# Hybrid decoder layer on one core: bank turn of the query projections, two scalars in the probability scaling, deferred last step of the output projection

## Chip, cores and metric

One core of one Trainium2 chip runs the whole program. The metric is the device time of one execution in microseconds (us), the median of several runs.

## What is computed

One decoder layer over 512 tokens of width 1024: a gated linear recurrence and a sparse attention in parallel, merged by two sigmoid gates, an output projection, an expert layer (16 experts of 16384 for each of 8 heads and token) and a gated embedding. The part that matters here, cut from the reference:

```
z_q, z_kv, z_ng, z_m = parts of rmsnorm(x) @ w_in
p_s = masked_softmax(q_rot @ k_s);  p_w = masked_softmax(q_rot @ k_w)
o_b = g0 * (p_c @ v_c) + g1 * (p_s @ v_s) + g2 * (p_w @ v_w)      # g = sigmoid(z_ng)
g_m = sigmoid(z_m).reshape(B, S, 2, D)
merged = g_m[:, :, 0] * y_a + g_m[:, :, 1] * (o_b @ w_b)
h = x + merged @ w_out
```

## The kernel before

Every float32 product is taken as three products of parts (hi x hi, hi x lo, lo x hi; `mm3`, lines 131 to 134). A part hi is a cast on ScalarE (line 126), a part lo a subtraction on VectorE or, for most weights, on GpSimd (line 129, both in `split`). Weights come in pieces of 512 KB through a ring of three raw buffers whose loads SyncE issues in a fixed order; a load waits until both readers of its buffer are done.

The order of the work is written out by hand, engine by engine, in the order of the Python code. Around the change it is this.

**Queries.** `gemm` projects eight pieces of queries. Each takes a PSUM bank from `bank`, whose tag goes round `"aaax"`: three banks under tag a, one (bank 3) under tag x. `ev_q` copies the piece on ScalarE and starts its rotation on VectorE (`rope`, lines 633 to 636, which read the bank); the scores against the compressed keys follow one piece later (line 658). During the pieces the first attention block takes two banks a for its scores.

**Merge gates.** `m_gemm` computes sixteen pieces of z_m as filler. It takes banks f and x in turn, eight steps of three matmuls to a piece. Its first twelve steps stand right behind the queries; the rest is spread between the steps of attention.

**Attention.** Sixteen blocks (128 tokens times two heads). For block n `att_a` makes scores, their maximum (line 754 or 751) and exponentials with sums (line 758); `att_a2` (lines 767 to 770) multiplies both branches of the probabilities P of one head by gate / sum. `att_b` of the block before, running at the same time, transposes its own P on TensorE (line 812), splits them into th and tl, and multiplies them with the values into bank o. Its last act is the split of o into ohi and olo (in the trace qhi and qlo, whose place they take). Head 0 of block n is scaled within `att_b(n - 1)`, head 1 behind it.

**Merge and output projection.** `gemm` with w_b gives eight pieces; `ev_yb` (lines 866, 867 and a split) makes mhi and mlo of each. Then w_out follows in four column groups q (lines 890 to 931): for each of four token tiles i, 16 matmuls with the hi weights over k = 0 to 7 (lines 914, 915), then for each i eight with the lo weights (line 898) and the addition to hres (line 900). Step k needs piece k of mhi and mlo. The weights of group q + 1 are cast behind tile 0.

```
def bank(name, tag="ax"):
    if tag == "ax":
        tag = "aaax"[turn[0] % 4]
        turn[0] += 1
    return ps.tile([128, 512], F32, name=name, tag=tag, bufs=NBK[tag])
```

Of the kernel before, what the change touches and what calls it, by code (L numbers as in the profile page):

```python
# [17 lines left out]
OP = mybir.AluOpType  # L18
# [5 lines left out]
NT = S // 128  # L24
KD = D // 128
# [69 lines left out]
def tile_hybrid(ctx, tc, a, out, dbg=None):  # L95
    nc = tc.nc
    V, A, T, G, SP = nc.vector, nc.scalar, nc.tensor, nc.gpsimd, nc.sync
# [15 lines left out]
    turn = [0]  # L113
# [7 lines left out]
    def f(ap):  # L121
        return ap.bitcast(F32)
# [21 lines left out]
    p1cm, p = enter(tc.tile_pool(name="p1", bufs=2, side="right"))  # L144
# [24 lines left out]
    ring = Ring(wp, nc, plan, 3)  # L169
# [367 lines left out]
    def pair_split(n, which, j, tiles):  # L537
        r = ring.get(n).rearrange("p (k c) -> p k c", k=KD)
        c = slice(j * 128, (j + 1) * 128)
        split(tiles[0][:, :, c], tiles[1][:, :, c], r, lo_eng[0])  # L540

    def pair(n):
        return [wp.tile([128, KD, 256], F32R, name="w8" + n + x, tag="w8") for x in "hl"]
# [32 lines left out]
    for br, n in enumerate(("vs", "vw")):  # L576
        hl = hls[br]
# [33 lines left out]
    gate = at.tile([128, NT, 24], F32, name="gate")  # L611
# [60 lines left out]
    def cmp_softmax_a(i, h0=0, h1=NH):  # L672
        s, m = pc[:, i, h0:h1], pm[:, 0, i, h0:h1]
        V.tensor_reduce(m, s, axis=AX.X, op=OP.max)
        V.tensor_tensor(s, s, m[:, :, None].to_broadcast([128, h1 - h0, NB]), op=OP.subtract)
        A.activation(s, s, AF.Exp, scale=SCALE)

    def cmp_softmax_b(i, h0=0, h1=NH):
        s, z, r = pc[:, i, h0:h1], pm[:, 1, i, h0:h1], pm[:, 2, i, h0:h1]
        V.tensor_reduce(z, s, axis=AX.X, op=OP.add)  # L680
        V.reciprocal(r, z)
        V.tensor_tensor(r, r, gate[:, i].rearrange("p (h b) -> p h b", b=3)[:, h0:h1, 0], op=OP.mult)
        if i == 0:
            V.tensor_scalar(r, r, cst[:, C_RM:C_RM + 1], None, op0=OP.mult)
        V.tensor_tensor(s, s, r[:, :, None].to_broadcast([128, h1 - h0, NB]), op=OP.mult)
# [76 lines left out]
    def att_a2(n, h):  # L762
        i, hp = blocks[n]
        W = (i + 1) * 128
        hh = hp * 2 + h
        P, st = Pt[n, h], stt.pop((n, h))
        V.reciprocal(st[:, 3], st[:, 2])
        V.tensor_tensor(st[:, 3], st[:, 3], gate[:, i, 3 * hh + 1:3 * hh + 3], op=OP.mult)
        for br in range(2):
            V.tensor_scalar(P[:, br, :W], P[:, br, :W], st[:, 3, br:br + 1], None, op0=OP.mult)  # L770

    def att_b(n, acts, more=None):
        i, hp = blocks[n]
        g = hp // 2
        oo = bank("o", "o")
        tiles = [(br, j) for br in range(2) for j in range(i + 1)]
        steps = [None] + [tiles[k:k + 2] for k in range(0, len(tiles), 2)]
        slots = [len(steps) + 2]
        half = slots[0] - max(1, int(slots[0] * PART))
        pend = []  # L780

        def gap():
            left = slots[0] - half
            if more and left == 0:
                acts.extend(more())
            for _ in range(-(-len(acts) // (left if left > 0 else slots[0]))):
                acts.pop(0)()
            slots[0] -= 1
            fill(1)

        def pv(k, last):
            js, th, tl = k
            if js is None:
                mm3(oo[:, :256], vchi[:NB, g], vclo[:NB, g], th[:NB, 0], tl[:NB, 0], True, last)
                return
            for m, (br, j) in enumerate(js):
                c = slice(g * 128, (g + 1) * 128)
                mm3(oo[:, :256], vhi[:, j, br, c], vlo[:, j, br, c], th[:, m], tl[:, m], False,
                    last and m == len(js) - 1)

        for js in steps:
            o = bank("pT", "t").rearrange("p (j x) -> p j x", j=2)
            th = p.tile([128, 2, 256], F32R, name="th", tag="th", bufs=3)
            tl = p.tile([128, 2, 256], F32R, name="tl", tag="tl", bufs=3)
            if js is None:
                for h in range(2):
                    T.transpose(o[:NB, 0, h * 128:(h + 1) * 128], pc[:, i, hp * 2 + h], ident)
                split(th[:NB, 0], tl[:NB, 0], o[:NB, 0])
            else:
                for m, (br, j) in enumerate(js):  # L810
                    for h in range(2):
                        T.transpose(o[:, m, h * 128:(h + 1) * 128], Pt[n, h][:, br, j * 128:(j + 1) * 128], ident)
                split(th[:, :len(js)], tl[:, :len(js)], o[:, :len(js)])
            gap()
            if len(pend) == 2:
                pv(pend.pop(0), False)
            pend.append((js, th, tl))
        while pend:
            gap()
            k = pend.pop(0)  # L820
            pv(k, not pend)
        oc = slice(hp * 2, hp * 2 + 2), slice(i * 128, (i + 1) * 128)
        split(ohi[:, oc[0], oc[1]], olo[:, oc[0], oc[1]], oo[:, :256].rearrange("p (h t) -> p h t", h=2))

# [7 lines left out]
        att_a2(0, 1)  # L832

    side += [lambda: None] * 3 + [att_0, lambda: cmp_softmax_a(0, 0, 4), lambda: cmp_softmax_b(0, 0, 4), att_02]
    gemm([("q", i, nhi, nlo, ev_q) for i in range(8)], nxt=[("m1", 0), ("m1", 1)])
    for _ in range(FILL0):
        next(fillg)
# [3 lines left out]
    for n in range(1, len(blocks) + 1):  # L841
        acts = []
        if n < len(blocks):
            acts = list(att_a(n, 0)) + [lambda: att_a2(n, 0)]
        cur[0] = blocks[n - 1][0]
        att_b(n - 1, acts, (lambda: att_a(n, 1)) if n < len(blocks) else None)
        if n < len(blocks):
            att_a2(n, 1)
            if n == 1:
                cmp_softmax_a(0, 4, 8)  # L850
                cmp_softmax_b(0, 4, 8)
            i, hp = blocks[n]
            if i + 1 < NT and hp in (2, 3):
                (cmp_softmax_a if hp == 2 else cmp_softmax_b)(i + 1)
# [15 lines left out]
    jobs = [("w_b", i, ohi, olo, ev_yb) for i in range(8)]  # L870
    gemm(jobs[:7], nxt=[("w_b", 7)])
    hl = pair("wo")
    for j in range(2):
        pair_split("w_out", None, j, hl)
    gemm(jobs[7:])

    p3cm, p = enter(tc.tile_pool(name="p3", bufs=2, side="left"))
    hres = at.tile([128, NT, D], F32, name="hres", tag="gm")
# [12 lines left out]
    for q in range(4):  # L891
        os = [bank("wo") for _ in range(NT)]
        nhl = None

        def wo_lo(i):
            ts = slice(i * 128, (i + 1) * 128)
            for k in range(KD):
                T.matmul(os[i][:, :256], mhi[:, k, ts], hl[1][:, k], start=False, stop=k == KD - 1)
            hv = hres[:, i, q * 256:(q + 1) * 256]
            V.scalar_tensor_tensor(hv, os[i][:, :256], 0.5, hv, op0=OP.mult, op1=OP.add)  # L900
            if q == 3:
                rms_stat(hres[:, i], i, x2s[:, i])
                rms_fin(i, i + 1)
                if i >= 1:
                    rms_apply(x2s[:, i - 1], hres[:, i - 1], i - 1, gB)
                if i >= 2:
                    to_T(x2s[:, i - 2], x2hi, x2lo, i - 2)

        if q < 3:
            nhl = pair("wo")  # L910
        for i in range(NT):
            ts = slice(i * 128, (i + 1) * 128)
            for k in range(KD):
                T.matmul(os[i][:, :256], mhi[:, k, ts], hl[0][:, k], start=k == 0, stop=False)
                T.matmul(os[i][:, :256], mlo[:, k, ts], hl[0][:, k], start=False, stop=False)
            if q == 3:
                wo_lo(i)
            if nhl and i == 0:
                for j in range(2):
                    r = ring.get("w_out", 2).rearrange("p (k c) -> p k c", k=KD)  # L920
                    A.copy(nhl[0][:, :, j * 128:(j + 1) * 128], r)
                    nhl.append(r)
        for i in range(NT):
            if q < 3:
                wo_lo(i)
            if nhl and i == 0:
                for j in range(2):
                    c = slice(j * 128, (j + 1) * 128)
                    G.tensor_tensor(nhl[1][:, :, c], nhl[2 + j], f(nhl[0][:, :, c]), op=OP.subtract)
        if q == 0:  # L930
            split(phl[:, 0], phl[:, 1], pw[:, 0].rearrange("p (k t) -> p k t", k=2), G, V)
        elif q < 3:
            split(wphl[:, 0, q - 1], wphl[:, 1, q - 1], pw[:, q], G, V)
        if q == 2:
            hi_eng[0] = V
            look([("wq", 0)])
        hl = nhl
# [654 lines left out]
```

## Time and profile before

| what | value |
|---|---|
| median of 3 runs | 1894.97 us (1893.92 to 1895.76) |
| the profiled execution's own time | 1896.81 us |
| its span in the trace | 1895.0 us |
| busy: TensorE, VectorE, ScalarE, GpSimd | 96%, 74%, 44%, 34% |
| queries / attention / w_b / w_out, about | 280 to 330 / 330 to 530 / 530 to 574 / 574 to 625 us |
| expert layer and end, about | 625 to 1895 us |

The chain that ended last runs over TensorE for 73% of the span. TensorE's queue is in order, so a matmul that waits holds all behind it. In the rows, PE is TensorE, PEld its weight load, DVE VectorE, ACT ScalarE, POOL GpSimd. A time in square brackets at the end of a row is how long the engine stood idle before it, and whose end it waited for.

### The profile page before, as it was taken

The page shows a single profiled execution, that of the slowest core. Times are in us where ns is not written, and L with a number is a line of the kernel's source. Part 1 is how long each engine was busy: PE and PEld are TensorE (multiplying, and loading weights), DVE is VectorE, ACT ScalarE, POOL GpSimd, SP SyncE. Part 2 cuts the span into 40 slices and gives each one's busy share as a digit, 9 for nine tenths or more (in the row PEclk, how much of TensorE's full clock was granted, in tenths as well). Part 3 has the DMA queues.
Part 4 walks back from the last instruction along what each step waited for, and adds up shares of the span by engine and source line. Part 5 has one row for each costly group of instructions (what it writes and reads, how often), then busy time and mean ns, then how long its engine had stood idle before and what let it go on. Part 6 is the DMA issues. An engine that isn't in the chain of part 4 may idle for free.

```text
span 1895.0 us, 26509 instructions
## 1 busy us (share of the span) xinstructions
PE 1819.3 (96%) x9817; PEld 1594.3 (84%) x9817; DVE 1401.5 (74%) x2658; ACT 840.3 (44%) x1274; POOL 648.8 (34%) x419
## 2 busy tenths in 40 slices
PE   7998999999999989999999999999999999999997
PEld 6777888777789879899999888888888899999986
DVE  6867607565633378999999967888888788888864
ACT  4464333344522434574674763333333333333443
POOL 3311454322135325335335321222222255556400
PEclk9999999899999999999999999999999999999999
DMA  4353232211015426697787998999999899999941
GB/s 171 105 183 97 89 101 67 67 56 45 23 67 178 190 87 202 233 365 257 275 331 258 335 357 298 355 358 352 347 355 353 304 338 324 348 337 350 363 178 45
DMA packets 179810, 433.29 MB, mean 229 GB/s; under 512 B 14560, under 2 KB 88032, under 8 KB 179680
## 3 DMA queue, kind: packets, MB, share of 16 engines
q1 hardware_dynamic: 119664, 241.96, 36.8%
q0 software_dynamic: 40288, 145.77, 21.5%
q10 hardware_dynamic: 19728, 43.86, 6.1%
q8 instruction: 77, 1.26, 0.3%
q14 instruction: 53, 0.43, 0.1%
HBM read 382.25 MB, written 49.28 MB: 228 GB/s over the span
## 4 chain that ended last, share of the span: by engine, by line
PE 73%; DVE 16%; ACT 4%; issue 4%; DMA 3%; POOL 0%; SPq 0%; DVEq 0%; ACTq 0%; POOLq 0%
PE va L132 9%; PE va L134 9%; PE va L133 9%; PE xu L134 7%; PE xu L132 7%; PE xu L133 7%; DVE ul L1087 2%; DVE oh L1259 2%; DVE gr L1288 1%; PE G L1236 1%; PE z_m L132 1%; PE z_m L133 1%; PE z_m L134 1%; DVE acc L1294 1%; PE sc L996 1%
## 5 line engine op out<-in xcount | busy, mean ns | idle before, releaser
L132 PE MATMUL xu<-x2hi,uh 128*128 128x384 f32 x1008 | 345.2, 342 | 4.7 <-ACT ac L1097 4.7
L134 PE MATMUL xu<-x2hi,ul 128*128 128x384 f32 x1008 | 340.6, 338 | 5.8 <-DVE ul L1087 5.8
L133 PE MATMUL xu<-x2lo,uh 128*128 128x384 f32 x1008 | 339.9, 337 | 0.0
L132 PE MATMUL va<-v,A 128*128 128x512 f32 x768 | 299.0, 389 | 1.5 <-ACT A L126 1.5
L134 PE MATMUL va<-v,A 128*128 128x512 f32 x768 | 298.8, 389 | 0.0
L133 PE MATMUL va<-v,A 128*128 128x512 f32 x768 | 298.8, 389 | 0.0
L1273 POOL DMA_INDIRECT gr<-in_peer_u,eidx x128 | 170.7, 1333 | 327.8 <-DVE gr L1288 250.5
L1273 POOL DMA_INDIRECT gr<-in_peer_v,eidx x128 | 187.8, 1467 | 267.5 <-DVE acc L1294 210.2
L126 ACT CAST v<-vring 128x1024 fp32r<-128x1024 f32 x128 | 134.7, 1052 | 262.7 <-issue 144.2
L129 DVE TENSOR_TENSOR v<-vring,v 128x1024 fp32r<-128x1024 f32 x128 | 156.5, 1223 | 67.8 <-ACT v L126 67.2
L132 PEld LDWEIGHTS xu<-x2hi,uh 128*128 128x128 f32 x1008 | 191.4, 190 | 7.0 <-ACT ac L1097 5.3
L134 PEld LDWEIGHTS xu<-x2hi,ul 128*128 128x128 f32 x1008 | 191.1, 190 | 6.8 <-DVE ul L1087 6.8
L133 PEld LDWEIGHTS xu<-x2lo,uh 128*128 128x128 f32 x1008 | 191.4, 190 | 1.6
L134 PEld LDWEIGHTS va<-v,A 128*128 128x128 f32 x768 | 144.1, 188 | 30.4 <-DVE A L129 0.3
L132 PEld LDWEIGHTS va<-v,A 128*128 128x128 f32 x768 | 144.1, 188 | 29.9 <-ACT A L126 1.8
L133 PEld LDWEIGHTS va<-v,A 128*128 128x128 f32 x768 | 144.1, 188 | 28.3
L1294 DVE SCALAR_TENSOR_TENSOR acc<-gr,dots,acc 128x1024 f32<-128x1024 f32 x128 | 164.0, 1281 | 2.2 <-DMA gr<-in_peer_v,eidx 0.7
L1288 DVE SCALAR_TENSOR_TENSOR gr<-gr,x2g 128x1024 f32<-128x1024 f32 x128 | 158.1, 1255 | 8.3 <-DMA gr<-in_peer_u,eidx 8.2
L1082 ACT CAST uh<-ur 128x1024 fp32r<-128x1024 f32 x126 | 132.6, 1053 | 59.6 <-ACT ac L1097 29.2
L1097 ACT ACTIVATE ac<-xu 128x384 f32<-128x384 f32 x128 | 63.8, 499 | 195.4 <-PE xu L134 185.1
L1087 DVE TENSOR_TENSOR ul<-ur,uh 128x1024 fp32r<-128x1024 f32 x100 | 121.4, 1220 | 17.8 <-PE xu L134 8.3
L1239 ACT ACTIVATE gst<-G 128x512 f32<-128x512 f32 x96 | 100.4, 1160 | 13.9 <-PE G L1236 13.6
(450 smaller groups left out, 3617.0 us busy)
## 6 DMA issues: line engine op xcount, KB each, us to landing
vring<-in_peer_v SPq DMA_DIRECT2D x128, 512.0 KB
ur<-in_peer_uT SPq DMA_DIRECT2D x126, 512.0 KB
gdram<-gst ACTq DMA_DIRECT2D x12, 2048.0 KB
gt<-gdram SPq DMA_DIRECT2D x32, 768.0 KB
xdram<-ac ACTq DMA_DIRECT2D x88, 192.0 KB
vring<-xdram SPq DMA_DIRECT2D x88, 192.0 KB
raw_m<-in_w_in SPq DMA_DIRECT2D x16, 512.0 KB
raw_rx<-in_w_in SPq DMA_DIRECT2D x8, 512.0 KB
```

What stands on the lines that cost most here:

```text
L126: A.copy(hi, src)
L129: (eng or V).tensor_tensor(lo, src, f(hi), op=OP.subtract)
L132: T.matmul(o, sh, mh, start=start, stop=False)
L133: T.matmul(o, sh, ml, start=False, stop=False)
L134: T.matmul(o, sl, mh, start=False, stop=stop)
L1082: A.copy(us[e][0], urs[e])
L1087: (G if search[0] else V).tensor_tensor(us[e][1], urs.pop(e), f(us[e][0]), op=OP.subtract)
L1097: A.activation(ac, o[:, :ND], AF.Gelu_apprx_tanh)
L1239: A.activation(gst[:, :, c:c + 4].rearrange("p a t -> p t a"), o.rearrange("p (t a) -> p t a", t=4), AF.Copy, scale=1.0 / GSC)
L1273: G.indirect_dma_start(out=r, out_offset=None, in_=tab, in_offset=bass.IndirectOffsetOnAxis(ap=eidx[:, j:j + 1], axis=0))
L1288: V.scalar_tensor_tensor(r, r, 1.0, x2g, op0=OP.mult, op1=OP.mult, accum_out=dots[:, j:j + 1])
L1294: V.scalar_tensor_tensor(acc, r, dots[:, j:j + 1], acc, op0=OP.mult, op1=OP.add)
```

## The change

Four edits.

1. `turn[0] = 3` ahead of the queries. Without it the count stands at a multiple of four there: pieces 3 and 7 of the queries take bank 3. With it pieces 0 and 4 do, piece 7 a bank a, and all later users of `"ax"` go round one place on.
2. `att_a2` drops the product gate / sum (line 768) and hands both scalars to the scaling instruction.
3. Head 1 of the next block is scaled by `att_a2` as `last()` ahead of the split of o, no longer behind it.
4. The lo part of the first w_out group leaves GpSimd for VectorE, behind the last `ev_yb`; and in that group tiles 0 and 1 run k = 0 to 6 first, and their k = 7 afterwards.

```diff
         V.reciprocal(st[:, 3], st[:, 2])
-        V.tensor_tensor(st[:, 3], st[:, 3], gate[:, i, 3 * hh + 1:3 * hh + 3], op=OP.mult)
         for br in range(2):
-            V.tensor_scalar(P[:, br, :W], P[:, br, :W], st[:, 3, br:br + 1], None, op0=OP.mult)
+            V.tensor_scalar(P[:, br, :W], P[:, br, :W], st[:, 3, br:br + 1],
+                            gate[:, i, 3 * hh + 1 + br:3 * hh + 2 + br], op0=OP.mult, op1=OP.mult)
...
+        if last:
+            last()
         oc = slice(hp * 2, hp * 2 + 2), slice(i * 128, (i + 1) * 128)
         split(ohi[:, oc[0], oc[1]], olo[:, oc[0], oc[1]], oo[:, :256].rearrange("p (h t) -> p h t", h=2))
...
+    turn[0] = 3
     gemm([("q", i, nhi, nlo, ev_q) for i in range(8)], nxt=[("m1", 0), ("m1", 1)])
...
-        att_b(n - 1, acts, (lambda: att_a(n, 1)) if n < len(blocks) else None)
+        att_b(n - 1, acts, *((lambda: att_a(n, 1), lambda: att_a2(n, 1)) if n < len(blocks) else ()))
         if n < len(blocks):
-            att_a2(n, 1)
...
+    wraw = []
     for j in range(2):
-        pair_split("w_out", None, j, hl)
+        wraw.append(ring.get("w_out").rearrange("p (k c) -> p k c", k=KD))
+        A.copy(hl[0][:, :, j * 128:(j + 1) * 128], wraw[j])
     gemm(jobs[7:])
+    for j in range(2):
+        c = slice(j * 128, (j + 1) * 128)
+        V.tensor_tensor(hl[1][:, :, c], wraw[j], f(hl[0][:, :, c]), op=OP.subtract)
...
+        if q == 0:
+            for i in range(2):
+                wo_hi(i, range(KD - 1))
+        for i in range(NT):
+            wo_hi(i, range(KD - 1 if q == 0 and i < 2 else 0, KD))
```

VectorE at the end of block 0 of attention, one piece of the difference (P the probabilities, ast their sums, tl a part of the transposed P, qlo the low part of the block's output):

```order
 L129 TENSOR_TENSOR tl<-pT,th 128x512
 L751 TENSOR_REDUCE ast<-s 128x2
 L755 TENSOR_SCALAR ast<-ast 128x2
 L705 SCALAR_TENSOR_TENSOR mA<-sm_2114,mA 128x512
+L767 RECIPROCAL ast<-ast 128x2
+L769 TENSOR_SCALAR P<-P,ast,gate 128x128 x2
 L129 TENSOR_TENSOR qlo<-o,qhi 128x2x128
-L767 RECIPROCAL ast<-ast 128x2
-L768 TENSOR_TENSOR ast<-ast,gate 128x2
-L770 TENSOR_SCALAR P<-P,ast 128x128 x2
 L674 TENSOR_REDUCE pcm<-pc 128x4
```

The scaling of head 1 stands ahead of the split of o instead of behind it, and one instruction is gone.

TensorE at the start of the output projection before, with numbers (wo_4703, wo_4704 and wo_4705 are token tiles 0, 1 and 2; 16 rows stand for tile 0 before the first of tile 1):

```order
L134 MATMUL z_w_b_4656<-qhi_2111,w8_4585 128x512
L914 MATMUL wo_4703<-w8woh_4646,mhi_4411 128x256
L915 MATMUL wo_4703<-w8woh_4646,mlo_4412 128x256
...
L914 MATMUL wo_4704<-w8woh_4646,mhi_4411 128x256
L915 MATMUL wo_4704<-w8woh_4646,mlo_4412 128x256
...
L914 MATMUL wo_4705<-w8woh_4646,mhi_4411 128x256
```

And in the change (wo_4671, wo_4672 and wo_4673 are tiles 0, 1 and 2), from the last of 14 + 14 rows with k = 0 to 6:

```order
L922 MATMUL wo_4672<-w8woh_4614,mhi_4379 128x256
L923 MATMUL wo_4672<-w8woh_4614,mlo_4380 128x256
L922 MATMUL wo_4671<-w8woh_4614,mhi_4379 128x256
L923 MATMUL wo_4671<-w8woh_4614,mlo_4380 128x256
L922 MATMUL wo_4672<-w8woh_4614,mhi_4379 128x256
L923 MATMUL wo_4672<-w8woh_4614,mlo_4380 128x256
L922 MATMUL wo_4673<-w8woh_4614,mhi_4379 128x256
```

The first matmul that needs piece 7 of mhi was number 15 of the stage and is now number 29.

VectorE behind the last piece of w_b, one piece of the difference (w8wol is the lo part of the first w_out group):

```order
 L129 TENSOR_TENSOR mlo<-sm_2114,mhi 128x512
-L900 SCALAR_TENSOR_TENSOR hres<-wo,hres 128x256 x4
+L882 TENSOR_TENSOR w8wol<-raw_w_out,w8woh 128x8x128 x2
+L907 SCALAR_TENSOR_TENSOR hres<-wo,hres 128x256 x4
 L128 CAST phl<-pw 128x1024
```

Two subtractions came in, behind the last mlo and ahead of the additions to hres; GpSimd has two fewer.

## Rows read from the trace of the kernel before

**Rows 1.** The page: span and TensorE's busy time.
```profile
span 1895.0 us, 26509 instructions
PE 1819.3 (96%) x9817; PEld 1594.3 (84%) x9817; DVE 1401.5 (74%) x2658; ACT 840.3 (44%) x1274; POOL 648.8 (34%) x419
```

**Rows 2.** TensorE's waits over the span: total us, times, longest.
```profile
PE z_m L132 <- DVE roper L636: 4.2, 1, 4.2
PE pT L812 <- DVE P L770: 3.8, 5, 1.4
PE s L132 <- ACT P L758: 3.1, 6, 0.8
PE wo L914 <- ACT mhi L126: 2.1, 1, 2.1
PE pT L812 <- DVE tl L129: 1.1, 5, 0.3
PE wo L915 <- DVE mlo L129: 0.3, 1, 0.3
```

**Rows 3.** Windows: us; busy PE, PEld, DVE, ACT, POOL; granted clock; DMA share, GB/s.
```profile
330.45:334.66 4.21, 0.00 (x1) 0.03 (x1) 4.10 (x11) 1.55 (x3) 0.30 (x2) 0.88 0.39 125
334.66:343.85 9.19, 9.19 (x29) 7.68 (x30) 2.38 (x6) 1.56 (x5) 6.23 (x3) 0.50 0.35 110
524.90:528.10 3.20, 3.20 (x16) 3.20 (x17) 1.38 (x2) 0.59 (x1) 0.00 (x0) 0.50 0.03 8
579.30:582.75 3.45, 3.45 (x19) 3.45 (x18) 0.00 (x0) 0.53 (x1) 0.00 (x0) 0.51 0.92 343
```

**Rows 4.** Timeline near 330 us: start, duration; TensorE's stalled matmul, VectorE's rotation.
```profile
334.66 0.77 PE L132 MATMUL z_m<-nhi,w 128*128 128x512 f32 x1 [4.21 <-DVE roper L636]
333.82 0.69 DVE L636 TENSOR_TENSOR roper<-z_q,cosT 128x512 f32<-128x512 f32 x1
```

**Rows 5.** Timeline of 401 to 407 us, ScalarE, VectorE and TensorE, one block's end.
```profile
401.95 0.20 ACT L758 ACTIVATION_READ_ACCUMULATOR P<-s,ast 128x1 f32 x1
402.67 0.69 DVE L705 SCALAR_TENSOR_TENSOR mA<-sm,mA 128x512 f32<-128x512 f32 x1 [1.64 <-ACT sm L701]
403.88 0.42 DVE L129 TENSOR_TENSOR qlo<-o,qhi 128x256 fp32r<-128x256 f32 x1 [0.52 <-ACT qhi L126]
404.41 1.63 DVE L768 TENSOR_TENSOR ast<-ast,gate 128x2 f32<-128x2 f32 x1
406.07 0.62 DVE L770 TENSOR_SCALAR P<-P,ast 128x256 f32<-128x256 f32 x2
406.48 0.55 PE L812 MATMUL pT<-cst,P 128*128 128x128 f32 x3 [1.32 <-DVE P L770]
```

**Rows 6.** Timeline of 569 to 595 us: all engines around the output projection.
```profile
569.56 0.69 DVE L867 TENSOR_TENSOR sm<-sm,mA 128x512 f32<-128x512 f32 x1
571.99 4.74 POOL L129 TENSOR_TENSOR w8wol<-raw_w_out,w8woh 128x1024 fp32r<-128x1024 f32 x2 [8.65 <-ACT w8woh L126]
575.06 2.22 DVE L867 TENSOR_TENSOR sm<-sm,mA 128x512 f32<-128x512 f32 x1
577.31 0.62 ACT L126 CAST mhi<-sm 128x512 fp32r<-128x512 f32 x1 [4.50 <-DVE sm L867]
586.02 3.79 PE L898 MATMUL wo<-w8wol,mhi 128*128 128x256 f32 x32
592.67 2.19 ACT L921 CAST w8woh<-raw_w_out 128x1024 fp32r<-128x1024 f32 x2 [12.85 <-DMA raw_w_out<-in_w_out]
```

**Rows 7.** VectorE's groups by form: busy us, mean ns, idle before.
```profile
L768 DVE TENSOR_TENSOR ast<-ast,gate 128x2 f32<-128x2 f32 x32 | 15.5, 485 | 1.1
L770 DVE TENSOR_SCALAR P<-P,ast 128x512 f32<-128x512 f32 x16 | 7.1, 484 | 0.3
L129 DVE TENSOR_TENSOR w<-raw_rg,w 128x1024 fp32r<-128x1024 f32 x8 | 9.8, 1226 | 0.3
```

**Rows 8.** One window of the expert stage, columns as in rows 3.
```profile
1200.00:1400.00 200.00, 200.00 (x884) 165.62 (x883) 163.43 (x218) 72.42 (x99) 49.33 (x48) 1.00 0.99 351
```

More of the change, by code (lines that the diff above doesn't have):

```diff
@@ L767, in att_a2, with att_b @@
         V.reciprocal(st[:, 3], st[:, 2])
-        V.tensor_tensor(st[:, 3], st[:, 3], gate[:, i, 3 * hh + 1:3 * hh + 3], op=OP.mult)
         for br in range(2):
-            V.tensor_scalar(P[:, br, :W], P[:, br, :W], st[:, 3, br:br + 1], None, op0=OP.mult)
-    def att_b(n, acts, more=None):
+            V.tensor_scalar(P[:, br, :W], P[:, br, :W], st[:, 3, br:br + 1],
+                            gate[:, i, 3 * hh + 1 + br:3 * hh + 2 + br], op0=OP.mult, op1=OP.mult)
+    def att_b(n, acts, more=None, last=None):
         i, hp = blocks[n]
@@ L910, in tile_hybrid, with wo_hi @@
             nhl = pair("wo")
-        for i in range(NT):
+        def wo_hi(i, ks):
             ts = slice(i * 128, (i + 1) * 128)
-            for k in range(KD):
+            for k in ks:
                 T.matmul(os[i][:, :256], mhi[:, k, ts], hl[0][:, k], start=k == 0, stop=False)
                 T.matmul(os[i][:, :256], mlo[:, k, ts], hl[0][:, k], start=False, stop=False)
+        if q == 0:
[3 more added lines that the diff above has]
+            wo_hi(i, range(KD - 1 if q == 0 and i < 2 else 0, KD))
             if q == 3:
```

## The prediction

> **What bounds the kernel now.** I read the page first: TensorE is busy for 96% of the span [rows 1], so time is won only where it stands still or runs at the lower of its two clock levels. Then I read TensorE's waits over the whole span. Six of them lie where the change works [rows 2]: 4.2 us of a merge gate matmul on the last query's rotation, 3.8 us of transposes on scaled probabilities, 3.1 us of scores on exponentials, 1.1 us of transposes on the split before, and 2.1 + 0.3 us of the output projection on the last merged piece. That is 14.6 us of standing. Then I read windows behind each wait for the granted clock [rows 3]: three stretches run at 0.50, that is at 1.2 instead of 2.4 GHz. They come behind the 4.2 us wait (9.19 us long), behind the last and longest wait on P (3.20 us) and behind the wait in the output projection (3.45 us). Work done at half speed takes twice its time, so half of each stretch is lost: 4.6 + 1.6 + 1.7 = 7.9 us. What can be won is about 14.6 + 7.9 = 22.5 us, or 1.2% of the span. No change from no change can be told below about 0.2% (3.8 us).
>
> **The bank of the last query.** The second merge gate piece takes bank 3, which holds query piece 7 until VectorE has done with it at 333.82 + 0.69 = 334.5; the matmul starts at 334.66 after 4.21 us [rows 4]. VectorE is behind there (4.10 of 4.21 us busy [rows 3]), and its work stays. With the turn moved, bank 3 holds piece 4, whose rotation stands three pieces earlier in VectorE's order, so this wait goes: 4.2 us. So does the slow stretch behind it, since TensorE no longer stands: 4.6 us. What is late next: the lo part of that gate piece's weights and the inputs of attention block 0, which hang on the same VectorE; TensorE now comes to them 4 us earlier, and those matmuls run in half the time. No row shows that wait. Below it is zero; above it could give back the 4.2 us, as VectorE's work does not shorten. Merge gate steps stand between each transpose and its use as cover, so I take 0.5 us. Gain: 4.2 + 4.6 - 0.5 = **8.3 us**. The banks of all later users go round by one place; they keep their order and distance, so I cost that at nothing.
>
> **The two scalars.** 32 instructions go. They hold VectorE for 15.5 us, 485 ns each in the mean [rows 7], but one of them took 1.63 us where the next scaling took 0.62 us for a pair [rows 5]: a two-column product costs no 1.6 us by itself, it waited. The Trainium skill (SBUF — State Buffer, section "Who interferes with whom", on the port pair that VectorE and GpSimd share) says that the pair is held for a whole instruction, that an operation with two inputs in SBUF waits for GpSimd there, and that a single-input operation in its fast mode does too. By that the wait passes on to the scaling, and only the short part of the 15.5 us is saved; by the row alone all of it would be. The sum needs neither: VectorE's time here counts only through TensorE's waits, which are costed next. No row shows a scaling with two scalars from memory. Below, it takes what one does, 484 ns for 512 columns [rows 7]; above, what a two-input operation of that shape takes, 0.69 us [rows 6]. The second scalar adds no tensor to read, so I take the lower end. The upper end costs 0.2 us for each of 64 at the widest, 13 us of VectorE, of which 15 blocks times two on TensorE's way make 6 us at most. This end goes into the range.
>
> **The scaling ahead of the split.** Rows 5 show one block's end. The sums of head 1 are there at 401.95 + 0.20 = 402.2, and VectorE is free at 402.67 + 0.69 = 403.4. Yet the scaling starts at 406.07, behind the split of o and the product; TensorE waits 1.32 us. In the new order the scaling starts at about 403.5 and ends at about 404.2, and TensorE wanted it at 406.48 - 1.32 = 405.2. All five such waits (3.8 us) go by this. The split then comes at about 404.2 instead of 403.88, and bank o is free 0.3 us later; the next use of o is several steps away, which hides it. Behind the split VectorE comes to the next block's maximum earlier by the reciprocal, the product and the scaling (1 us or more), and that maximum feeds the exponentials for which the scores wait (3.1 us, at most 0.8 each) and the split of the first transpose (1.1 us). They could all go or none; I take half: 2.1 us. The slow stretch of 3.20 us stands behind the last of the waits on P, and goes with it: 1.6 us. Gain: 3.8 + 2.1 + 1.6 = **7.5 us**, between 3.8 and 9.6.
>
> **The output projection.** GpSimd's two subtractions fill 571.99 to 576.73 [rows 6]. Beside them the last addition of `ev_yb` took 2.22 us where the one before took 0.69. Without them it takes 0.69 again, so the last mhi comes 1.5 us earlier. Then 14 more matmuls stand ahead of the first that needs it; 32 take 3.79 us, so 14 take 1.7 us [rows 6]. Cover and earlier piece together are 3.2 us against waits of 2.1 + 0.3, so both go, and with them the slow stretch (1.7 us): **4.1 us**. The price is on VectorE and in the queue of SyncE. Two subtractions of 1.23 us [rows 7] stand behind mlo and end near 579.6, while their first use comes behind 64 matmuls (64 x 0.12 = 7.6 us from 574). VectorE stands idle there. The raw buffers come free later: the first behind the first subtraction, near 578.3, not near 574.4; behind that load in SyncE's queue stand hres and all that follows, near 1 us later than now and half a megabyte more at 343 GB/s [rows 3], 1.5 us. The casts that waited for loads until 592.67 and end at 594.9 then end near 596.4. Group 2 of the projection now starts at 586.02 + 3.79 + 96 x 0.12 = 601.3, and would start near 597: the slack is used up, a wait of 0 to 1 us. Ends: 2.4 - 1.0 and 4.6; I keep 4.1, as the casts for that group come in order and the first half is early.
>
> **The sum.** 8.3 + 7.5 + 4.1 = 19.9 us off the profiled execution's 1896.81 us gives 1876.9. That execution lies 1.8 us above the median of the runs, 1894.97, so the median forecast is 1894.97 - 19.9 = **1875.0 us**.
>
> **Rivals.**
> - *The waits go, the speed does not come back, and half of what follows stays.* Then 4.2 + 3.8 + 2.4 = 10.4 us are won: 1884.6. For it: VectorE is behind at 334 us, and TensorE runs into it. Against it: each slow stretch stands right behind a long standstill.
> - *Given back later.* In the expert stage the DMA engines are 99% busy [rows 8]. If transfers set the pace there, an earlier start wins little: 1893 to 1895. Against it: TensorE is busy for 200.00 of 200 us in that window, and the rings start their loads by the program's progress, so they move along.
> - *Slower.* The scaling with two scalars in memory leaves VectorE's fast path altogether, each taking c us more. Its place is head 1 at each block's end, where two of them stand between the sums and TensorE, in 15 blocks. To lose the 20 us and 3.8 more, 30 c must pass 23.8, so it decides from c = 0.8 us; at c = 1.0 the time is 1875 + 30 = 1905. The nearest rows give 0 to 0.2 us. The Trainium skill (DVE: scalar operands, raw-bit mode, write accounting and state across instructions, section "Scalar operands") says that a scalar read through a pointer takes no second tensor stream; no run here shows two.
> - *The change does not free the bank.* If another holder of bank 3 were late, 8.3 us would be missing: 1883.3. Piece 4 and the count of the turns speak against it.
>
> **How the numbers follow.** The forecast has 0.70, the first rival and the missing bank together 0.20, given back 0.05, slower 0.03, and 0.02 is for a larger gain. The low end is all that can be won (22.5 us) and one slow stretch elsewhere of some 3 us less: 1869. The high end is the first rival's 1884.6, taken at 1884. Within it lie the upper price of the scaling (6 us) and of the loads (1 us). Faster by over 0.2%: 0.92; within: 0.05; slower: 0.03.
>
> **What would show it.** In the new profile no z_m matmul waits on the rotation, and the clock stays at 1.00 from 330 to 345 us and behind the output projection's start; the waits of transposes on P are gone or below 0.5 us together; the last addition of `ev_yb` takes 0.69 us; the scaling of 512 columns takes 0.48 to 0.69 us; the attention ends about 16 us earlier and the projection about 20, and that lead is the same at the end of the expert stage. The forecast is wrong if the lead shrinks behind 625 us, if slow stretches stay, or if a new wait of several us stands in block 0 or at group 2.

## The result and the profile after

The changed kernel took 1881.34 us in the median of 4 runs (1877.56 to 1883.07) beside 1894.74 us for the kernel before (1893.92 to 1895.76): 13.4 us less, ratio 0.9922, 95% interval 0.9904 to 0.9939. The forecast was 1875.0 us, 19.9 us less, with a range of 1869 to 1884. Run again later beside the experiments (e0_after), the same kernel took 1884.04 us against 1894.45, ratio 0.9955, interval 0.9940 to 0.9970. By these ratios the gain is 14.8 us in the first comparison and 8.5 in the second: the sign was right, the size too large.

The page of the changed kernel, as in [rows 1]:

```profile
span 1881.3 us, 26477 instructions
PE 1811.3 (96%) x9817; PEld 1586.6 (84%) x9817; DVE 1405.0 (75%) x2628; ACT 840.0 (45%) x1274; POOL 643.6 (34%) x417
```

TensorE's busy time fell by 8.0 us although it does the same work: that is mostly work that had run at half speed. VectorE's rose by 3.5 us although 32 instructions went and only two subtractions of 1.22 us came. TensorE's waits from 270 to 640 us (us in total, times, longest), to set beside [rows 2]:

```profile
PE pT L812 <- DVE P L769: 2.1, 2, 1.3
PE pT L812 <- DVE tl L129: 1.5, 2, 0.9
PE wo L922 <- ACT w8woh L935: 1.4, 1, 1.4
PE s L132 <- ACT P L758: 0.8, 1, 0.8
PE z_q L132 <- ACT mA L648: 0.7, 1, 0.7
PE o L133 <- DVE tl L129: 0.6, 1, 0.6
```

The z_m wait of 4.2 us is gone and so are the two of the projection on mhi and mlo. Three kinds are new: a query piece on `mA`, the projection's group 2 on its weights, and o on tl. Windows, columns as in [rows 3]: the first two are those of [rows 3], the others the end of the attention and the projection up to group 2.

```profile
330.45:334.66 4.21, 4.21 (x23) 3.35 (x22) 4.15 (x8) 3.08 (x5) 1.82 (x1) 1.00 0.27 73
334.66:343.85 9.19, 8.90 (x47) 6.96 (x47) 6.15 (x9) 1.91 (x7) 6.74 (x3) 1.00 0.23 81
506.00:518.10 12.10, 11.51 (x87) 10.46 (x86) 8.51 (x17) 5.99 (x13) 0.00 (x0) 1.00 0.01 1
562.00:569.54 7.54, 7.54 (x65) 7.53 (x64) 4.34 (x5) 1.57 (x2) 0.00 (x0) 1.00 0.29 98
569.54:586.20 16.66, 15.24 (x131) 15.04 (x129) 5.05 (x10) 3.15 (x3) 8.25 (x4) 1.00 0.89 336
```

The granted clock is 1.00 in all: the three slow stretches are gone. Where the new waits stand (timeline: start, duration):

```profile
275.12 0.50 PE L132 MATMUL z_q<-nhi,w 128*128 128x512 f32 x1 [0.67 <-ACT mA L648]
345.22 0.39 PE L133 MATMUL o<-tl,vv 128*128 128x256 f32 x1 [0.57 <-DVE tl L129]
347.81 2.36 POOL L129 TENSOR_TENSOR w<-raw_m,w 128x1024 fp32r<-128x1024 f32 x1 [4.96 <-ACT w L126]
348.27 2.24 DVE L769 TENSOR_SCALAR P<-P,ast,gate 128x128 f32<-128x128 f32 x2
350.31 0.59 PE L812 MATMUL pT<-cst,P 128*128 128x128 f32 x3 [1.35 <-DVE P L769]
360.70 0.58 PE L812 MATMUL pT<-cst,P 128*128 128x128 f32 x3 [0.77 <-DVE P L769]
586.20 0.38 PE L922 MATMUL wo<-w8woh,mhi 128*128 128x256 f32 x1 [1.42 <-ACT w8woh L935]
```

The fourth row is the one to see: two scalings of 128 columns, begun 0.46 us behind a GpSimd subtraction and done 0.34 us behind its end, took 2.24 us. VectorE's groups by form:

```profile
L769 DVE TENSOR_SCALAR P<-P,ast,gate 128x512 f32<-128x512 f32 x16 | 8.0, 543 | 0.3
L769 DVE TENSOR_SCALAR P<-P,ast,gate 128x128 f32<-128x128 f32 x12 | 8.3, 733 | 0.2
```

A scaling of 128 columns takes longer in the mean than one of 512. The product's 15.5 us [rows 7] did not go; the five forms of the scaling took 25.0 us before and take 38.8 us now, so 1.7 us are saved. The Trainium skill (SBUF — State Buffer, section "Who interferes with whom") has the port pair of VectorE and GpSimd held for a whole instruction, and by it the wait passes on to the scaling, as the prediction told; the trace agrees.

### The profile page after: what moved, and what is told of

Its sections match the earlier page's. It is cut to its first block, busy times and chain, and to the rows that moved or that the text cites. A ratio compares the mean times of both kernels' runs of the same rounds, so it can differ in the third digit from the quotient of the medians.

```text
span 1881.3 us, 26477 instructions
## 1 busy us (share of the span) xinstructions
PE 1811.3 (96%) x9817; PEld 1586.6 (84%) x9817; DVE 1405.0 (75%) x2628; ACT 840.0 (45%) x1274; POOL 643.6 (34%) x417
## 4 chain that ended last, share of the span: by engine, by line
PE 70%; DVE 16%; ACT 4%; issue 4%; DMA 4%; POOL 0%; SPq 0%; DVEq 0%; ACTq 0%; POOLq 0%
PE va L134 9%; PE va L133 9%; PE va L132 9%; PE xu L134 7%; PE xu L132 7%; PE xu L133 7%; DVE ul L1101 2%; DVE oh L1273 2%; DVE gr L1302 2%; PE G L1250 1%; DVE P L769 1%; DMA w1buf<-in_cmp_w 1%; DVE acc L1308 1%; PE z_w_a L134 1%; PE z_w_b L133 1%
## 5 line engine op out<-in xcount | busy, mean ns | idle before, releaser
L1253 ACT ACTIVATE gst<-G 128x512 f32<-128x512 f32 x96 | 100.3, 1158 | 13.5 <-PE G L1250 13.2
```

Source lines behind the costliest of these rows:

```text
L1253: A.activation(gst[:, :, c:c + 4].rearrange("p a t -> p t a"), o.rearrange("p (t a) -> p t a", t=4), AF.Copy, scale=1.0 / GSC)
```

## The experiments

Each ran beside the kernel before on the same chip; the sets ran on four chips, so kernels of different sets are compared by their ratios. The stages are read from one trace of each, between first matmuls: queries from z_q to z_m, attention from z_m to z_w_b, w_out from wo to z_wq, rest from z_wq to the end (w_b takes 44.0 us in all of them). Times are us; the ratio is to the kernel before.

| kernel | z_q starts | queries | attention | w_out | rest | median | ratio, 95% interval |
|---|---|---|---|---|---|---|---|
| before | 273.7 | 51.0 | 205.5 | 64.1 | 1256.8 | 1894.7 | 1 |
| after | 275.1 | 51.1 | 191.8 | 62.7 | 1256.6 | 1881.3 | 0.9922 (0.9904 to 0.9939) |
| e1_turn | 276.3 | 51.2 | 200.1 | 64.2 | 1257.6 | 1892.7 | 0.9993 (0.9984 to 1.0002) |
| e2_att | 277.9 | 51.0 | 193.3 | 64.1 | 1255.5 | 1886.7 | 0.9958 (0.9946 to 0.9970) |
| e3_wo | 273.7 | 51.0 | 205.2 | 64.1 | 1256.4 | 1893.3 | 0.9989 (0.9979 to 1.0000) |
| e4_tt | 276.1 | 51.2 | 193.8 | 61.4 | 1255.3 | 1885.2 | 0.9952 (0.9940 to 0.9964) |
| e0_after | 275.9 | 51.1 | 191.8 | 62.1 | 1254.1 | 1884.0 | 0.9955 (0.9940 to 0.9970) |
| e56 | 274.6 | 55.0 | 188.7 | 61.0 | 1254.8 | 1880.2 | 0.9928 (0.9914 to 0.9942) |
| e7_fill | 276.0 | 51.1 | 194.3 | 62.2 | 1255.4 | 1886.3 | 0.9963 (0.9948 to 0.9977) |
| e8_lock | 278.2 | 51.1 | 194.1 | 63.5 | 1255.8 | 1884.7 | 0.9956 (0.9941 to 0.9970) |
| e9_m01 | 275.9 | 51.1 | 189.9 | 63.1 | 1258.0 | 1883.5 | 0.9941 (0.9927 to 0.9955) |
| e10_best | 278.7 | 51.1 | 189.8 | 61.0 | 1257.0 | 1878.6 | 0.9912 (0.9895 to 0.9928) |
| e11_bm01 | 275.6 | 51.0 | 201.0 | 64.1 | 1254.9 | 1893.5 | 0.9991 (0.9980 to 1.0001) |
| e12_m4 | 276.0 | 51.1 | 188.2 | 61.6 | 1255.8 | 1876.5 | 0.9894 (0.9878 to 0.9911) |

The time ahead of the queries and the rest spread over 5 and 4 us, although no edit aims at them: in part half-speed stretches fall there at other places from trace to trace. That is not all of it, as before and e11_bm01 start the queries 1.9 us apart with a slow stretch of the same length ahead of them. So a stage tells more than a median.

The granted clock over the whole span, on record for every run to 0.001, parts the gain. The span times what that clock lacks to 1 is the time lost to the lower level, an estimate. In the mean of its runs beside e0_after the kernel before loses 20.7 us, and e0_after 15.4: of the 9.6 us between their mean spans 5.3 are clock and 4.2 all else. For e2_att 0.5 us are clock and 7.0 all else. For e1_turn 2.9 us are won by the clock and 1.6 lost by all else.

**Each part alone, and the whole without its two scalars.**

e1_turn, on the kernel before:

```diff
+    turn[0] = 3
     gemm([("q", i, nhi, nlo, ev_q) for i in range(8)], nxt=[("m1", 0), ("m1", 1)])
```

> The kernel before with the moved turn alone (the bank order of the queries, the merge gate and everything behind). Theory: the standstill of 4.2 us at the second merge gate piece and the half-speed stretch behind it (4.6 us) both go, the first query piece now waits 0.7 us on the projection's last evacuation, and about 1 us of new waits stands in attention block 0: 1894.9 - 7 = 1888 us, with waits of transposes on scaled probabilities no smaller than before. Rival (the standstill goes, but the clock falls at another place, or VectorE's backlog takes it back in block 0): 1894.9 - 3.5 = 1891.5 or later. On the pitch of the output projection (384 matmuls 0.1134 us apart before, 0.1177 us with the whole change): if the bank order makes it, it is 0.1177 us here; if the tile order does, 0.1134 us.

Measured: 1.3 us gained (3.0 to -0.4). The theory fell in size, the rival is nearer. In its trace the attention is 5.4 us shorter, but that trace has no slow stretch there and the one before has two; the medians show how little is sure. The z_m standstill went, and these came:

```profile
346.56 0.38 PE L133 MATMUL o<-tl,vv 128*128 128x256 f32 x1 [0.65 <-DVE tl L129]
351.91 0.55 PE L812 MATMUL pT<-cst,P 128*128 128x128 f32 x3 [1.61 <-DVE P L770]
362.25 0.55 PE L812 MATMUL pT<-cst,P 128*128 128x128 f32 x3 [0.83 <-DVE P L770]
```

With one scalar and the old order the waits of blocks 0 and 1 are 3.1 us, no shorter than with the whole change; so the moved bank brings them, not the new scaling (e2_att, next, has none of them). A standstill costs more than its bracket says: between the same transposes this kernel took 11.8 us (338.24 to 350.02) where the one before took 10.0 (344.06 to 354.06), with waits of 0.31 and 0.65 us in it.

e2_att: edits 2 and 3 of the change on the kernel before, diff as shown there.

> The kernel before with the two scalars in one instruction and the scaling ahead of the split, bank order and output projection untouched. Theory: the waits on scaled probabilities fall from 3.8 us to below 2, the half-speed stretch of 1.6 us behind the last of them goes, and the scalings themselves now take 0.5 to 0.65 us each because they wait for GpSimd's splits in place of the product that went: 1894.9 - 6.5 = 1888.5 us, the 4.2 us standstill at the merge gate unchanged. Rival (the waits in blocks 0 and 1 come from the scaling and not from the earlier start that the bank order gives): the 1.35 and 0.77 us waits of the first two blocks stand here too, and the gain is 4 us, 1891.

Measured: 8.0 us gained (5.7 to 10.2), as the theory had it and twice the rival. No transpose waits for P any more, neither in blocks 0 and 1 nor later. The old standstill is there, and behind it something else than before (timeline, and two windows):

```profile
338.82 0.57 PE L132 MATMUL z_m<-nhi,w 128*128 128x512 f32 x1 [4.14 <-DVE roper L636]
```

```profile
334.68:338.82 4.14, 0.00 (x0) 0.03 (x1) 4.06 (x10) 1.55 (x3) 0.30 (x1) 1.00 0.40 127
338.82:342.40 3.58, 3.58 (x9) 2.79 (x10) 0.46 (x1) 0.62 (x1) 3.58 (x2) 0.53 0.00 0
```

The same standstill of the same matmul, with the same code up to there, was followed by 9.19 us at half speed in the kernel before [rows 3] and by 3.58 us here. In e3_wo, next, it is 4.21 us long and some 8.9 us at 0.50 follow. How much the clock takes behind a standstill differs from execution to execution.

What the moved bank adds to this is best seen from the first transposes of block 0 to those of block 3, first in the changed kernel, then here:

```profile
337.03 0.60 PE L812 MATMUL pT<-cst,sm 128*128 128x128 f32 x4
369.61 0.60 PE L812 MATMUL pT<-cst,P 128*128 128x128 f32 x4
345.52 0.60 PE L812 MATMUL pT<-cst,sm 128*128 128x128 f32 x4
373.82 0.60 PE L812 MATMUL pT<-cst,P 128*128 128x128 f32 x4
```

That is 32.6 us against 28.3, and 28.2 in the kernel before: 4.3 us more, about as much as the standstill of 4.14 us that the moved bank took away.

e3_wo: edit 4 alone, diff as shown in the change.

> The kernel before with the output projection's part alone (deferred last contraction step, lo part of the first weights on VectorE behind the last gate piece). Theory A (the slower pitch of 0.1177 us comes with the tile order of the projection or with VectorE's subtractions): waits of 2.1 + 0.3 us and 1.7 us of half speed go, 1.4 us at group 2 and 1.6 us of pitch come, 1894.9 - 1.1 = 1893.8 us. Theory B (the pitch comes from the bank order): the pitch stays at 0.1134 us and the gain is 2.7 us, 1892.2. In both group 2 waits 1 to 1.5 us on ScalarE's cast of its weights.

Measured: 2.1 us gained (4.0 to 0), but in its trace nothing: w_out took 64.1 us. The wait at group 2 came as expected, and the clock fell behind it:

```profile
598.62 0.39 PE L920 MATMUL wo<-w8woh,mhi 128*128 128x256 f32 x1 [1.91 <-ACT w8woh L933]
```

```profile
600.00:602.00 2.00, 2.00 (x11) 0.50 0.53 207
```

The slow stretch was not removed, it moved with the wait. On the pitch (the time from the start of one matmul to that of the next) neither theory holds: it was 0.1177 us up to that standstill and 0.1134 us behind it.

e4_tt: the change without edit 2 (lines 768 to 770 as before).

> The whole change without its two scalars: the product with the gate is its own instruction again, and the scaling has one scalar. Theory (what the two scalars save is the short part of the product, 0.1 to 0.15 us per head, as the wait for GpSimd falls on whichever of the two comes first): within 1.5 us of the whole change, 1881.5 to 1883, with the long durations on the product's line and scalings of 0.48 us. Rival (the two-scalar scaling is what makes the new waits in blocks 0 and 1): those waits go, and it is 2 us faster than the whole change, 1879. Second rival (the whole 0.48 us of the product counts at every block's end): 15 x 0.48 = 7 us slower, 1888.

Measured: ratio 0.9952 beside 0.9955 (e0_after) and 0.9922 for the whole change: the theory, though 2 us later than the numbers given. In the attention the two scalars are worth 2.0 us, by one trace without them and two with them, so the second rival, 7 us, is out; the ratios show no difference from e0_after. Group 2 waited 0.39 us here, though edit 2 does not reach it. The first rival is out too: the waits of blocks 0 and 1 stand here (0.65, 1.60, 1.02 us).

**What makes the new waits.**

e0_after: the changed kernel, no edit.

> The changed kernel once more, unedited, on the chip and in the rounds of the runs beside it, as their yardstick. Both theories: 1880 to 1885 us; the waits of blocks 0 and 1 (0.57, 1.35, 0.77 us) and the 1.4 us at group 2 of the output projection stand again. What it tells by itself is the clock and the pitch: if half-speed stretches and the pitch of the projection's matmuls (0.1134 or 0.1177 us) are set by the kernel, they stand where they stood; if they are drawn anew in each execution, they differ while the waits stay.

Measured: all waits from the queries to group 2 within 0.03 us of the first trace. The pitch of the projection's second half was 0.1134 us where the first trace had 0.1177 throughout; the switch came at the wait of group 2. So the kernel alone does not set the pitch.

e56:

```diff
-    turn[0] = 3
+    turn[0] = 2
...
+    p3cm, p = enter(tc.tile_pool(name="p3", bufs=2, side="left"))
+    gB = bcast(p.tile([128, D], F32, name="gffnB", bufs=1), a["g_ffn"], D)
+    pw = p.tile([128, 3, D], F32, name="pw", bufs=1)
+    SP.dma_start(pw[:, 0], a["pT"])
+    SP.dma_start(pw[:, 1:3], a["ple_wp"].rearrange("(k p) c -> p k c", p=128))
     jobs = [("w_b", i, ohi, olo, ev_yb) for i in range(8)]
...
```

The same five lines go from their place around the loads of hres.

> The whole change, with the turn set to 2 in place of 3 (the second merge gate piece then takes a bank that query piece 5 held, and the first query piece no longer the one that the projection's last piece holds), and with the loads of the last norm's scale and of the per-layer weights (2 MB) issued before the last gate pieces instead of behind the residual. Theory (each of the two waits has the cause I read): the 0.7 us at the first query piece goes, no wait on a rotation comes back, the 1.4 us at group 2 falls below 0.3 us; together 2 to 3 us with the restarts behind them, 1879. Rival A (the residual's own 2 MB hold the weights up, not what stands behind it): group 2 still waits about 1 us. Rival B (VectorE's backlog takes what the first query piece gains): the waits of blocks 0 and 1 grow from 2.7 to 3.4 us, and the time is that of the changed kernel.

Measured: group 2 no longer waits (w_out 61.0 us, 1.1 to 1.7 us less), so rival A is out: the 2 MB of norm scale and per-layer weights held the weights up. ScalarE's cast of those weights begins 15.6 us into the stage, where it began at 21.9 in the changed kernel (583.92 us):

```profile
577.87 1.05 ACT L935 CAST w8woh<-raw_w_out 128x1024 fp32r<-128x1024 f32 x1 [6.14 <-DMA raw_w_out<-in_w_out]
```

The three traces with the early loads show no wait at group 2, the seven with edit 4 and without them 0.39 to 2.45 us. The first query piece no longer waits either, and of the waits of blocks 0 and 1 one of 0.76 us is left. But a wait on a rotation, which the theory had ruled out, came in their place:

```profile
302.46 0.50 PE L132 MATMUL z_q<-nhi,w 128*128 128x512 f32 x1 [2.15 <-DVE roper L636]
```

Behind the two banks that block 0's scores take, this turn gives the next piece the bank of the piece just before it. Behind that wait 3.40 us ran at 0.50. Queries and attention together took 243.7 us, beside 242.9 and 243.0 in the two traces of the changed kernel: the turn only chooses where TensorE meets a late VectorE.

e7_fill: `FILL0 = 18` for 12.

> The whole change with 18 instead of 12 merge gate steps between the last query piece and attention block 0 (six steps of 0.69 us moved forward, none added). Theory (blocks 0 and 1 wait because VectorE's backlog is some 3 us longer than the cover): the waits of 0.57, 1.35 and 0.77 us there fall below 0.3 us together; the cover runs out 4 us earlier at the end of the attention, where new waits of 1 to 4 us come: between 1 us faster and 1 us slower than the changed kernel. Rival (the scaling itself is late in these blocks, whatever the cover): the 1.35 and 0.77 us stay.

Measured: nearer the rival. More cover did not help:

```profile
353.29 0.33 PE L812 MATMUL pT<-cst,P 128*128 128x128 f32 x1 [0.75 <-DVE P L769]
373.53 0.59 PE L812 MATMUL pT<-cst,P 128*128 128x128 f32 x3 [1.21 <-DVE P L769]
```

The waits moved with the steps, and the attention became 2.4 us longer. My reading, VectorE's backlog alone, fell. The new one: TensorE meets scalings that have just run into a subtraction on GpSimd. Here GpSimd began one at 350.74 and at 371.02 us, and scalings begun at 350.83 and 371.54 us took 2.40 and 1.94 us.

e8_lock:

```diff
+    lo_eng[0] = V
     for _ in range(FILL0):
         next(fillg)
...
+    lo_eng[0] = G
     jobs = [("w_b", i, ohi, olo, ev_yb) for i in range(8)]
```

> The whole change with the low parts of the merge gate's weights subtracted on VectorE instead of GpSimd, so that GpSimd does nothing while the attention runs. Theory (the scalings' 543 to 733 ns are waiting for GpSimd's instruction of 2.3 us): without it the scaling with two scalars takes 0.54 us or less at 512 columns and 0.31 to 0.36 at 128 in the mean, that is the one-scalar duration and 0.06 us. Rival (two scalars are slow by themselves at few columns): 0.65 to 0.73 us at 256 and 128 columns stay. Its time is expected to be longer, as VectorE gets 16 subtractions of 1.2 us (20 us) more: 1881 to 1895.

Measured, VectorE's groups:

```profile
L769 DVE TENSOR_SCALAR P<-P,ast,gate 128x512 f32<-128x512 f32 x16 | 8.0, 544 | 0.3
L769 DVE TENSOR_SCALAR P<-P,ast,gate 128x256 f32<-128x256 f32 x16 | 5.9, 410 | 0.3
L769 DVE TENSOR_SCALAR P<-P,ast,gate 128x128 f32<-128x128 f32 x12 | 3.6, 344 | 0.2
```

GpSimd has nothing to do from 341 us to the end of the attention. Then 128 columns take 344 ns, not 733: the theory. Against one scalar (484 ns at 512 columns [rows 7]; 350 and 283 ns at 256 and 128 in the same view) the second scalar costs 0.06 us whatever the width. No transpose waits for P in any block. The price was one wait of 2.96 us at 343 us, where VectorE is behind, and the slow stretch after it (6.08 us at 0.50); scores waited for exponentials 2.0 us, and group 2 waited 2.45 us.

e9_m01 and, on the kernel before, e11_bm01:

```diff
-        split(w[:, 0], w[:, 1], r, lo_eng[0], hi_eng[0])
+        split(w[:, 0], w[:, 1], r, V if key in (("m1", 0), ("m1", 1)) else lo_eng[0], hi_eng[0])
```

> The whole change, with the low parts of the first two merge gate pieces' weights subtracted on VectorE (1.2 us each) instead of GpSimd (2.4 us each); the other fourteen stay on GpSimd. Theory (VectorE is late in blocks 0 and 1 because, during the last two query pieces, its small instructions wait behind those two subtractions: 2.3 us at a 128x4 product, 1.0 us before it, 3.8 us at the first scaled pair): these fall to about 0.2, 0.2 and 1.5 us, VectorE is some 3 us earlier in spite of 2.4 us more work, the waits of 0.57, 1.35 and 0.77 us fall below 0.7 us together, and the attention is 3 us shorter than in the changed kernel: 1881 beside 1884 us. Rival (VectorE is late by its own work): the waits grow by 2 us, 1886.

> The kernel before, nothing of the change, with those two subtractions on VectorE. Theory (the 4.2 us standstill on the last query's rotation is the same backlog of VectorE, and the bank only decides where it is met): the standstill falls from 4.2 to about 1.3 us without any bank moved, and no waits come in blocks 0 and 1: 3 us by the waits and 0 to 4 us by the clock, 1888 to 1891.5 us. Rival (the bank is the cause): the standstill stays at 4 us or more, 1894 to 1897.

The timeline of the kernel before shows what these two look for: two small instructions of VectorE beside GpSimd's.

```profile
321.29 2.41 POOL L129 TENSOR_TENSOR w<-raw_m,w 128x1024 fp32r<-128x1024 f32 x1
321.39 2.33 DVE L684 TENSOR_SCALAR pcm<-pcm,cst 128x4 f32<-128x4 f32 x1
327.09 1.29 POOL L637 TENSOR_TENSOR roper<-roper,ropeb 128x512 f32<-128x512 f32 x1 [3.40 <-DVE ast L767]
327.25 3.58 DVE L770 TENSOR_SCALAR sm<-sm,ast 128x128 f32<-128x128 f32 x2
328.34 2.41 POOL L129 TENSOR_TENSOR w<-raw_m,w 128x1024 fp32r<-128x1024 f32 x1
```

And of e9_m01:

```profile
323.67 0.23 DVE L684 TENSOR_SCALAR pcm<-pcm,cst 128x4 f32<-128x4 f32 x1
328.37 1.67 DVE L769 TENSOR_SCALAR sm<-sm,ast,gate 128x128 f32<-128x128 f32 x2
349.08 0.58 PE L812 MATMUL pT<-cst,P 128*128 128x128 f32 x3 [1.20 <-DVE P L769]
```

A product of 128 x 4 numbers falls from 2.33 to 0.23 us; the one before it keeps its 1.02 us, as it waits for GpSimd's part of a rotation. VectorE comes to the last rotation 2.0 us earlier (334.09 instead of 336.08 us in e0_after), the wait of o on tl goes, the attention is 2.0 us shorter. The waits of 1.20 and 0.78 us on P stay, which the expectation did not have, and by its ratio, 0.9941, the kernel cannot be told from e0_after. In e11_bm01, with no bank moved, the old standstill halves, and no waits came in blocks 0 and 1:

```profile
334.54 0.49 PE L132 MATMUL z_m<-nhi,w 128*128 128x512 f32 x1 [2.23 <-DVE roper L636]
```

So the bank was where TensorE met VectorE; about half of VectorE's lateness was time spent waiting for GpSimd. Its time, 1.7 us less (3.8 to -0.2), says little: the clock fell there as well.

**Both repairs, and the last two waits.**

e10_best: e9_m01 with the early loads of e56, at the turn of the change.

> The run before, and the early loads of the last norm's scale and the per-layer weights. Theory: the two repairs add up, no wait at group 2 (1.4 us and its restart): 3 + 1.8 us below the changed kernel of the same chip, 1879, and 15 us below the kernel before. Rival (the clock gives back what the waits gave): within 1.5 us of the changed kernel.

Measured: ratio 0.9912, 1878.6 us, w_out 61.0 us, group 2 without a wait. They add up. Two waits on P are left (1.19 and 0.75 us). Ahead of the first stand these scalings, with GpSimd beside them:

```profile
349.44 2.37 POOL L129 TENSOR_TENSOR w<-raw_m,w 128x1024 fp32r<-128x1024 f32 x1 [4.89 <-ACT w L126]
349.96 2.19 DVE L769 TENSOR_SCALAR P<-P,ast,gate 128x128 f32<-128x128 f32 x2
```

e12_m4: `key[1] in (0, 1, 4, 5)` of m1 on VectorE, and the early loads.

> The run before (both repairs), and two more merge gate pieces, the fifth and the sixth, subtracted on VectorE, just ahead of the scalings of head 1 in blocks 0 and 1. Theory (the waits of 1.2 and 0.8 us that are left there are collisions: these scalings take 2.2 us instead of 0.6 because GpSimd started on such a subtraction just before them, 0.5 us ahead in each block): the scalings there take 0.6 us, and as VectorE first needs 1.2 us for the subtraction, the two waits fall together from 2.0 to about 0.6 us; the attention is 1.5 us shorter and the time 1877. Rival (VectorE's amount of work makes these waits): they stay or grow by 1.2 us each, 1880 to 1881.

Measured:

```profile
348.04 0.60 DVE L769 TENSOR_SCALAR P<-P,ast,gate 128x128 f32<-128x128 f32 x2
348.44 0.59 PE L812 MATMUL pT<-cst,P 128*128 128x128 f32 x3 [0.38 <-DVE P L769]
```

The scalings take 0.60 us instead of 2.19, one wait of 0.38 us is left of 1.94, although VectorE had 2.5 us more to do: the collision was the cause. At 1876.46 us (1874.75 to 1878.37, 4 runs) against 1896.28 this is the fastest median of all, 20.1 us below the kernel before (16.9 to 23.1), with an interval that overlaps that of e10_best; its attention is 3.6 us shorter than that of the changed kernel.

## Why the prediction was right in sign and too large

From the start of the queries to that of z_wq the traces give 364.5 us before and 349.6 after: 15.0 of the 19.9 (attention 13.7 of 15.8, projection 1.4 of 4.1). The rest of the program, which the change does not touch, kept that lead (1256.8 and 1256.6 us), so "given back later" did not happen. Of the signs that the prediction named, the z_m wait is gone, the clock is 1.00, the last addition takes 0.69 us and the scaling of 512 columns 0.54. But the attention ends 12.1 us earlier and not 16, the projection 13.5 and not 20, and waits on P of 2.1 us are left, where 0.5 was the bound.

The first median lies in the range and the second, 1884.04 us, at its upper end, beside the first rival's 1884.6. That nearness is luck: this rival has the speed stay away, and in both traces of the changed kernel it is back.

- **The bank, 8.3 us.** The standstill and the slow stretch behind it went, as said. The step that failed is "Merge gate steps stand between each transpose and its use as cover, so I take 0.5 us". The text had named the bound, 4.2 us given back, and all of it was: the runs show waits of 0.22 + 0.57 + 1.35 + 0.77 = 2.9 us in blocks 0 and 1, and 4.3 us by the time between the same transposes, which holds what else the standstills cost. Of these 4.3 us e9_m01 and e12_m4 won back 1.8 and 3.5 by taking subtractions off GpSimd (30.8 and 29.1 us between the same transposes), so most of it was VectorE waiting for GpSimd and not VectorE's own work. "I cost that at nothing" for later users failed too: the first query piece now stands right behind the holder of bank 3 and waits 0.67 us. And the 4.6 us of clock are not a fixed price: behind the same standstill e3_wo shows some 9 us of slow clock again, but e2_att 3.58, and over the runs of e1_turn the clock gave back 2.9. On top of edits 2 and 3 the whole change has 1.5 us less attention; alone the turn gained 1.3 us. The first rival's reason saw this ("VectorE is behind at 334 us, and TensorE runs into it").
- **The two scalars, nothing.** Right in the price: 0.06 us each, near the lower end, against 0 to 0.2. The wait passed on to the scaling. "Nothing" was a little too low: by e4_tt they are worth 2.0 us of attention in the traces.
- **The scaling ahead of the split, 7.5 us.** Right: with the two scalars 8.0 us measured; without them it was not run on the kernel before. Waits of transposes on P outside blocks 0 and 1 are gone, and the waits on exponentials and splits fell from 4.2 us to 2.3 in the later blocks and 0.6 us at o, near the half that was taken. The 1.6 us of clock in this term are not fixed either: e1_turn has the same last wait on P (1.38 us), and the clock stayed at 1.00 behind it.
- **The output projection, 4.1 us.** The last addition to `ev_yb` takes 0.69 us, mhi is there in time, the clock is 1.00. The step that failed is "a wait of 0 to 1 us ... I keep 4.1": group 2 waited 1.42 us, as 2 MB of other loads stood ahead of its weights in SyncE's queue. Counted from the first matmul of the stage, its casts ended at 20.7 us before and at 24.1 after: 3.4 us later, where the prediction had 1.5. And the slower pitch, on 384 matmuls, cost 384 x 0.0043 = 1.7 us in that trace. The stage gained 1.4 us, in e0_after 2.0.

Of the 4.9 us that are missing in the traces, 2.7 lie in the projection and 2.1 in the attention. There the bank gave back 3.8 us more than the 0.5 forecast, and edits 2 and 3 must have won some 1.7 us more than forecast, by difference. The remainder between the traces and the medians lies outside these stages: 0.67 us is the wait ahead of the first query matmul, part is clock stretches. What decides their place was not tried and stays open.

## What to carry to other kernels

A standstill on a buffer can be a late engine in disguise: moving the buffer moves the place where that engine is met, so ask first why it is late, and look for tiny instructions with long durations beside another engine's long ones. Price the slow clock behind a standstill as a range over several traces, not by the one at hand, and part a gain of medians into clock and the rest by the granted clock of the runs. When a wait is taken away, follow the engine that was waited for through the next two stages, and the load queue past the work that moves.

## What the hardware showed that was not expected

- The same 4.1 to 4.2 us standstill was followed by some 9 us at 1.2 GHz in two traces (before, e3_wo) and by 3.58 us in a third (e2_att). Behind the 1.42 and 1.45 us at group 2 the clock stayed at 2.4 GHz in both traces of the changed kernel, behind 1.91 us in e3_wo it fell, and behind 2.45 us in e8_lock it stayed (1.00 over the next 7.53 us).
- At 2.4 GHz, matmuls of 256 columns ran 0.1134 or 0.1177 us apart, in the same program in one execution and not in the other. In e0_after, e3_wo and e4_tt the change from one to the other came at or near the standstill of group 2; in e8_lock it came at 578.7 us and in the kernel before at 574.7 us, with no idle time ahead of it. 32 of them take 3.79 us at the one pitch [rows 6] and 3.93 us at the other, here in e12_m4:

```profile
566.84 3.93 PE L905 MATMUL wo<-w8wol,mhi 128*128 128x256 f32 x32
```

- Two GpSimd instructions in a row held up two scalings in a row. The row at 327.25 us, 3.58 us long, is a pair: the first took 1.21 us and ended 0.09 us behind GpSimd's first instruction, the second took 2.44 us and ended 0.08 us behind GpSimd's second.
